# A row-wise maximum on one core: VectorE out of the opening barrier, one wait kept, a tail of 38 segments

## Chip, cores, metric

One core of a Trainium2 chip. The metric is device time in microseconds (us). The profile's span (first to last instruction of the kernel) is some 2.6 us shorter than the time.

## The reference

```python
def setup_inputs():
    return {"x": np.random.randn(8192, 8192).astype(np.float32)}

def reference(x):
    return np.linalg.norm(x, ord=np.inf, axis=1)
```

For a matrix, this norm along axis 1 is the largest absolute value of each row: 268 MB in, 32 KB out, one comparison per element.

## The kernel before

It walks through 32 tiles of 128 partitions with 16384 columns, two rows to a partition, in three buffers. The first 24 are loaded and reduced whole. The next seven ("the tail") are loaded in pieces of the widths in `TAIL`, and each piece is reduced as it lands, cut at the row's end (column 8192). The last tile has twelve pieces; its partial results are written beside the last piece of each row, so that one reduction closes the row.

```python
TAIL = [
    [4736, 11648],
    [12928, 3456],
    [7040, 9344],
    [9344, 7040],
    [3584, 6784, 6016],
    [5376, 4864, 1792, 4352],
    [4096, 3584, 3200, 2944, 2560],
]
LAST = (
    [(0, w) for w in (2176, 1792, 1792, 1664)]
    + [(1, w) for w in (1664, 1408, 1280, 1152, 1024, 896)]
    + [(0, 768), (1, 768)]
)
# ... cut: segments(), the passes on the finished program ...
def drop_implied_waits(nc):
    # ... cut: for loads on SP ...
        elif i.engine == dve and own and len(waits) > 1:
            past = max(behind.get((s.id, s.wait_value), 0) for s in waits)
            if past >= own:
                insts[n] = rewait(i, [s for s in waits if s.id != counter])
# ... cut ...
    for i, loads in enumerate(TAIL):
        t = sbuf.tile([P, W + PAD], F32, tag="t")
        # ... cut ...
        for j, w in enumerate(loads):
            nc.sync.dma_start(out=t[:, at : at + w], in_=x_t[i][:, at : at + w])
            at += w
            for _, b, c, n in [s for s in todo if s[0] == j]:
                k, lo = seen[b], b * cols + c
                absmax(part[:, i * B + b, k : k + 1], t[:, lo : lo + n])
                seen[b] += 1
```

The program opens with a barrier of all engines; one pass moves the first load ahead of it. The last two reductions each wait for two things, a load and VectorE's own counter; the first of these waits is an instruction of its own. In the trace of before the record of the last but one such wait is at 621.90 us (0.02 us long), while the reduction ahead still runs, to 622.20. What handles waits is called VectorE's sequencer here.

## Time and profile before

| | before |
|---|---|
| time, first three runs | 627.36, 627.47, 627.99 us |
| span of the profiled run | 624.7 us |
| load queue, share of 16 DMA engines | 99.6% |
| VectorE busy | 552.6 us (88%), 64 reductions |
| waits of VectorE for loads, 24 bulk tiles / tail | 70.6 us / 0.7 us |

The prediction shows the lines. In a timeline line the columns are: start, duration of the group, engine, source line, operation, output and input, shape of the first, count, and in brackets the idle time ahead of it and what ended it.

### The profile page before, as it was taken

Reading aid. Unit: us, or ns where it says so; the run is one execution under the profiler, and the core shown is the slowest. Engines: PE = TensorE matmul, PEld = TensorE weight load, DVE = VectorE, ACT = ScalarE, POOL = GpSimd, SP = SyncE. Lnnn points to the kernel's source line nnn. Section 1 sums busy time; section 2 is a strip of 40 time slices with the busy share of each in tenths; the row PEclk is TensorE's granted clock in tenths of the full one; section 3 lists DMA queues with packets and bytes.
Section 4 is the critical chain, followed back from the end, with each engine's and each line's share of the span. In section 5 each row is a group of like instructions: output and inputs, shape, how many; then the busy total and the mean of one; then the engine's idle time right before and its main releaser. Section 6 shows DMA issues by size and latency. Waiting matters only on the chain.

```text
span 624.7 us, 154 instructions
## 1 busy us (share of the span) xinstructions
DVE 552.6 (88%) x64; POOL 0.3 (0%) x5
## 2 busy tenths in 40 slices
DVE  0588988889988889888898888988889999999999
POOL 0000000000000000000000000000000000000000
DMA  9999999999999999999999999999999999999998
GB/s 403 457 415 457 415 449 424 441 432 411 462 403 470 403 470 403 453 420 449 424 445 428 415 457 403 470 403 470 403 427 446 424 430 438 418 434 429 425 425 340
DMA packets 8849, 268.47 MB, mean 430 GB/s; under 512 B 1680, under 2 KB 1680, under 8 KB 3216
## 3 DMA queue, kind: packets, MB, share of 16 engines
q1 hardware_dynamic: 8064, 268.44, 99.6%
q10 hardware_dynamic: 784, 0.02, 0.1%
q14 instruction: 1, 0.01, 0.0%
HBM read 268.44 MB, written 0.03 MB: 430 GB/s over the span
## 4 chain that ended last, share of the span: by engine, by line
DMA 64%; DVE 36%; issue 0%
DMA t<-in_x_dram 64%; DVE r_bulk L262 22%; DVE part L262 11%; DVE t L262 3%; DVE r_tail L262 0%
## 5 line engine op out<-in xcount | busy, mean ns | idle before, releaser
L262 DVE TENSOR_REDUCE r_bulk<-t 128x2 f32<-128x16384 f32 x24 | 413.3, 17220 | 70.6 <-DMA t<-in_x_dram 70.6
L262 DVE TENSOR_REDUCE part<-t 128x1 f32<-128x8192 f32 (+18 forms) x27 | 121.5, 4569 | 0.7 <-DMA t<-in_x_dram 0.7
L262 DVE TENSOR_REDUCE t<-t 128x1 f32<-128x1792 f32 (+7 forms) x10 | 16.2, 1687 | 0.0
L262 DVE TENSOR_REDUCE r_tail<-t 128x1 f32<-128x772 f32 (+1 forms) x2 | 1.8, 944 | 0.0
L262 DVE TENSOR_REDUCE r_tail<-part 128x14 f32<-128x42 f32 x1 | 0.2, 186 | 0.0
L259 POOL MEMSET part<- 128x42 f32 x1 | 0.1, 134 | 0.0
L343 POOL MEMSET const-bfloat16-1.0<- 128x1 bf16 x1 | 0.1, 102 | 0.0
L343 POOL MEMSET const-uint8-127<- 128x1 uint8 x1 | 0.1, 102 | 0.0
L343 POOL MEMSET const-float32-0.0<- 128x1 f32 x1 | 0.1, 98 | 0.2 <-issue 0.2
L343 POOL MEMSET const-float32-1.0<- 128x1 f32 x1 | 0.1, 98 | 0.0
## 6 DMA issues: line engine op xcount, KB each, us to landing
t<-in_x_dram SPq DMA_DIRECT2D x2, 4672.0 KB, 37.6
t<-in_x_dram SPq DMA_DIRECT2D x2, 3520.0 KB, 36.3
t<-in_x_dram SPq DMA_DIRECT2D x1, 6464.0 KB, 36.7
t<-in_x_dram SPq DMA_DIRECT2D x1, 5824.0 KB, 40.4
t<-in_x_dram SPq DMA_DIRECT2D x2, 1792.0 KB, 34.4
t<-in_x_dram SPq DMA_DIRECT2D x1, 3392.0 KB, 37.4
t<-in_x_dram SPq DMA_DIRECT2D x1, 3008.0 KB, 44.1
t<-in_x_dram SPq DMA_DIRECT2D x1, 2688.0 KB, 34.1
```

The costliest lines, as they stand in the source:

```text
L259: nc.gpsimd.memset(part[:], 0.0)
L262: return nc.vector.reduce_max(out=o, in_=i, axis=X, apply_absolute_value=True)
L343: nc = _bacc.Bacc("TRN2", target_bir_lowering=False, num_devices=1)
```

## The change

Its intent, as the diff reads, is to take from VectorE its part in the opening barrier (an announcement and a wait), and one segment of the tail (a segment is what one reduction takes; 39 before, 38 after). One wait that had been dropped as implied stays. The tail's widths are shuffled so that in the sixth tile a piece ends on the row's end.

```diff
 TAIL = [
-    [4736, 11648],
-    [12928, 3456],
+    [12672, 3712],
+    [4992, 11392],
     [7040, 9344],
     [9344, 7040],
     [3584, 6784, 6016],
-    [5376, 4864, 1792, 4352],
+    [3968, 4224, 4736, 3456],
     [4096, 3584, 3200, 2944, 2560],
 ]
@@ drop_implied_waits (cut: its bookkeeping lines, which go too)
-        elif i.engine == dve and own and len(waits) > 1:
-            past = max(behind.get((s.id, s.wait_value), 0) for s in waits)
-            if past >= own:
-                insts[n] = rewait(i, [s for s in waits if s.id != counter])
@@ new pass, run last
+def open_without_vector(nc):
+    dve, pool = mybir.EngineType.DVE, mybir.EngineType.Pool
+    main = nc.main_func.blocks[0]
+    out = []
+    for i in main.instructions:
+        kind = type(i).__name__
+        if i.engine == dve and kind in ("InstDrain", "InstEventSemaphore"):
+            continue
+        # ... cut: POOL's wait and release of the barrier count one less ...
+        out.append(i)
+    main.instructions = out
```

## The prediction

> **What bounds the kernel now.** I read the page first, top down: engines, slices, queues, chain, groups. The kernel streams 268.44 MB of float32 through 128-partition tiles of 16384 columns (24 "bulk" tiles of one load each, 8 "tail" tiles of several loads) and takes the largest absolute value per row on VectorE (DVE).

> ```profile
> span 624.7 us, 154 instructions
> DVE 552.6 (88%) x64; POOL 0.3 (0%) x5
> ...
> DMA  9999999999999999999999999999999999999998
> ...
> q1 hardware_dynamic: 8064, 268.44, 99.6%
> HBM read 268.44 MB, written 0.03 MB: 430 GB/s over the span
> ```

> To see here: in all 40 slices the DMA engines are at 90% or more, and the load queue alone keeps the sixteen engines 99.6% busy. VectorE has 12% to spare. The span is bytes divided by DMA rate, plus a short head and a short end.

> Second, the groups with shapes kept apart, and one stretch of the timeline, for the two speeds:

> ```profile
> L262 DVE TENSOR_REDUCE r_bulk<-t 128x2 f32<-128x16384 f32 x24 | 413.3, 17220 | 70.6 <-DMA t<-in_x_dram 70.6
> L262 DVE TENSOR_REDUCE part<-t 128x1 f32<-128x8192 f32 x4 | 34.7, 8681 | 0.2 <-DMA t<-in_x_dram 0.2
> L262 DVE TENSOR_REDUCE part<-t 128x1 f32<-128x1152 f32 x2 | 2.7, 1342 | 0.0
> ...
> 22.03 17.22 DVE L262 TENSOR_REDUCE r_bulk<-t 128x2 f32<-128x16384 f32 x1 [22.03 <-DMA t<-in_x_dram]
> ...
> 466.67 17.22 DVE L262 TENSOR_REDUCE r_bulk<-t 128x2 f32<-128x16384 f32 x1 [2.14 <-DMA t<-in_x_dram]
> ```

> To see here: from the first bulk reduction at 22.03 to the 24th at 466.67 there are 23 tiles in 444.64 us, 19.33 us each; VectorE needs 17.22 and waits about 2.1 us per tile for the DMA.

> Third, the tail, where the change lies:

> ```profile
> 483.81 17.33 DVE L262 TENSOR_REDUCE part<-t 128x1 f32<-128x4736 f32 x3
> 501.32 86.61 DVE L262 TENSOR_REDUCE part<-t 128x1 f32<-128x8192 f32 x18 [0.19 <-DMA t<-in_x_dram]
> 588.47 17.57 DVE L262 TENSOR_REDUCE part<-t 128x1 f32<-128x4096 f32 x6 [0.54 <-DMA t<-in_x_dram]
> 605.96 2.41 DVE L262 TENSOR_REDUCE t<-t 128x1 f32<-128x2176 f32 x1
> 608.28 0.19 DVE L262 TENSOR_REDUCE r_tail<-part 128x14 f32<-128x42 f32 x1
> 608.38 13.82 DVE L262 TENSOR_REDUCE t<-t 128x1 f32<-128x1792 f32 x9
> 622.12 1.81 DVE L262 TENSOR_REDUCE r_tail<-t 128x1 f32<-128x772 f32 x2
> 623.96 0.35 SPq L324 DMA_DIRECT2D out_dram<-r_tail  x1
> ```

> To see here: VectorE is nearly always busy here because it began the tail 17 us behind the data, but it still waits for data twice: 0.19 us at 501.32 and 0.54 us at 588.47. After 588.47 it runs to the end almost without a gap, one small load after another. So the end hangs on when the load at 588.47 and those after it land, and then on VectorE work after that. Work saved on VectorE before 588.47 cannot reach the end.

> Fourth, the waits of the queue that issues the loads, for the opening barrier, and the start of the chain of waits:

> ```profile
> SPq L343 <- PEq L343: 0.2, 1, 0.2
> ...
> 0.73 0.07 issue
> 0.80 40.50 DMA t<-in_x_dram
> ```

> To see here: the only wait of the issuing queue in the opening barrier is 0.2 us, put down to TensorE's sequencer and not to VectorE. It then issues the second load at 0.80.

> [...]8.389 MB per 19.33 us is 434 GB/s in the bulk. Nothing in the change can raise that. [...](8681 - 1342) ns over (8192 - 1152) columns is 1.042 ns a column[...], so a reduction costs about 1.042 ns per column plus 1342 - 1201 = 141 ns. [...]a reduction that reads what VectorE has just written starts at 608.28 and the next at 608.38, 0.10 us later. [...] The kernel before has two reductions (the last two) that wait for both a load and VectorE's own counter; the gap before each is at most 0.2 us.

> **The change part by part.**

> *1. VectorE out of the opening barrier.* Two small VectorE sequencer instructions go (its report and its wait), and the collector on POOL counts one fewer. The last to report was not VectorE, so the barrier opens at the same time[...]. Even the whole 0.80 us would gain nothing in the load stream: the first load is issued at 0.00, ahead of the barrier, and keeps all engines busy for about 20 us, so the second only has to be there by about 20. VectorE's first work is at 22.03. Effect on the end: 0.

> *2. A wait kept.* The pass no longer drops VectorE's wait on its own counter where the load waited for had itself been issued behind that count. The code puts such a wait on the first reduction of the last tile (it writes partial results into a reused buffer), so about 605.96. The count it asks for was reached when the buffer's former tile was done, about 570. [...] This stretch is the one that sets the end, so a cost would count fully. [...]

> *3. Tail splits.* The number of loads per tile does not change (2, 2, 2, 2, 3, 4, 5 and 12), nor the bytes. Only tiles 1, 2 and 6 have other widths. With about 1.19 us per 1000 columns (19.5 us per 16384):

> Tile 1, first load 12672 instead of 4736: lands at 466.65 + 15.0 = 481.7, still before VectorE is free at 483.81. Three segments as before. Effect 0.

> Tile 2, first load 4992 instead of 12928: it lands 9.4 us earlier, so the wait of 0.19 at 501.32 goes. VectorE comes to be 0.19 earlier, until the second load of tile 4, which it took up at 535.92 straight after other work; that load lands near there, so the 0.19 should come back as a wait there or later.

> Tile 6, segments 3968, 4224, 4736, 3456 instead of 5376, 2816, 2048, 1792, 4352: the new cut falls exactly on the row's end (3968 + 4224 = 8192), so four reductions do what five did. An extra segment costs (17.33 - 17.22)/2 = 0.055 us from tile 1, or (17.57 - 17.22)/5 = 0.07 from tile 7, because most of the 141 ns overlaps the neighbour. So 0.06 us less VectorE work. Loads land at about 568.3, 573.4, 579.1 and 583.2; reductions of 4.28, 4.54, 5.08 and 3.74 us then end near 587.7, against 583.25 + 4.68 = 587.93 before. The next load lands near 588.45 in both, since the bytes before it are the same. So the wait before it grows from 0.54 to about 0.75 and the end does not move.

> Sum: [...]about 0 us of 627.5.

> **The rivals.**

> *The kept wait holds VectorE.* [...] For it: there is no slack after 588.47. Against it: the count is some 35 us old.

> *VectorE sets the end throughout the tail.* Then both the 0.06 of a segment and the 0.19 of tile 2 would come off: about 627.2. For it: 156.5 us busy of the last 158.7. Against it: the wait of 0.54 at 588.47, which swallows both.

> *Other load sizes starve or slow the DMA.* Loads are issued when a buffer of the three comes free, and late in the tail when an earlier load of the same semaphore has landed. If one came too late, the stream would have a hole; a hole of 1 us would be 628.5. Against it: issue to landing of tail loads is mostly 30 to 45 us, so one or two whole tiles always stand in the queue; the buffers' releases move by less than 0.3 us. [...]

> *The barrier held the launch.* If VectorE in unprofiled runs reaches its first instruction late, leaving it out gains some tenths: 627.0 to 627.3. The trace doesn't show this, but time minus span (627.3 - 624.7) is not seen in the profile at all.

> **Range and chances.** Predicted 627.4 us. The three runs of before spread over 0.63 us, more than everything above adds up to[...]. A range of 626.6 to 628.2 is 627.4 plus or minus 0.8. 2% is 12.5 us: no part of the change has a path to that in either direction. Only an accident[...] could, so 0.5% for faster and 1% for slower.

> **What would show it right or wrong.** Right: DMA at 9 in all slices, 430 GB/s; bulk reductions still 19.33 us apart; no wait near 501; a wait of about 0.7 just before the 4096-column reduction, still at about 588.5; four reductions in tile 6; the last reductions at about 622.1 and 623.0; the second load issued within 0.05 us of 0.80. Wrong: the 4096-column reduction starting before 588.3 or after 588.8 (the load stream moved), a gap over 0.1 us around 606 (the kept wait costs), or a last reduction that starts other than 34.5 us after it.

The sum came to about 0 us of 627.5. Two terms, barrier and tail, were 0 each.

## The result, and the profile after

| | before | after |
|---|---|---|
| time, median of 6 fast runs | 627.62 us (627.36 to 628.06) | 627.42 us (627.25 to 628.14) |
| span of the profiled run | 624.7 us | 624.7 us |

The ratio is the mean time of one kernel's fast runs over that of the other's in the same rounds, so not quite the ratio of these medians: 0.9999, with a 95% interval of 0.9986 to 1.0012. That is the same time. A second set of five runs of the same text (run 6 below) gave 0.9996 (0.9984 to 1.0009).

So the forecast of 627.4 held. But its own list of signs did not. The page of after, engines, memory and groups (columns as in the prediction; line numbers have moved by 18):

```profile
span 624.7 us, 152 instructions
...
HBM read 268.44 MB, written 0.03 MB: 430 GB/s over the span
...
L280 DVE TENSOR_REDUCE part<-t 128x1 f32<-128x8192 f32 (+19 forms) x26 | 121.4, 4739 | 0.5 <-DMA t<-in_x_dram 0.5
...
L280 DVE TENSOR_REDUCE r_tail<-t 128x1 f32<-128x772 f32 (+1 forms) x2 | 1.8, 954 | 0.2 <-DVE t L280 0.2
```

One reduction fewer, 0.5 us of waiting for loads where before had 0.7, and a line that before did not have: a reduction near the end stood idle for 0.2 us, which the view puts down to VectorE itself. VectorE's timeline of after, the stretches that answer to those in the prediction:

```profile
466.75 17.22 DVE L280 TENSOR_REDUCE r_bulk<-t 128x2 f32<-128x16384 f32 x1 [2.13 <-DMA t<-in_x_dram]
...
536.01 8.69 DVE L280 TENSOR_REDUCE part<-t 128x1 f32<-128x8192 f32 x1 [0.31 <-DMA t<-in_x_dram]
...
588.20 17.61 DVE L280 TENSOR_REDUCE part<-t 128x1 f32<-128x4096 f32 x6 [0.23 <-DMA t<-in_x_dram]
605.73 2.41 DVE L280 TENSOR_REDUCE t<-t 128x1 f32<-128x2176 f32 x1
...
622.14 1.82 DVE L280 TENSOR_REDUCE r_tail<-t 128x1 f32<-128x772 f32 x2 [0.16 <-DVE t L280]
```

Measured from the start of the last bulk reduction, so that the stream's early history drops out, the 4096-column reduction starts after 588.20 - 466.75 = 121.45 us. In before it was 588.47 - 466.67 = 121.80. The load stream is 0.35 us ahead, although not a byte less is loaded. The load just ahead of this one was still level: its last completion came 116.52 us after the start of the last bulk reduction in both. Then the last but one reduction starts 0.16 us after the one ahead of it has ended, where back-to-back reductions start 0.08 us *before* the other's recorded end (in before 621.13 + 1.07 = 622.20 against 622.12). That is 0.24 us lost. Gain and loss nearly cancel: the last reduction starts 156.32 us after the last bulk one in before (622.99) and 156.26 in after (623.01).

Both show in the DMA view of a short window, which the prediction had not asked for. The page of before already had a queue named "instruction", with one packet. The DMA view of before, 586 to 588 us:

```profile
q1 hardware_dynamic: 69, 0.80, 96.6%
q14 instruction: 1, 0.01, 1.0%
```

and of after, the same window, then 622 us to the end:

```profile
q1 hardware_dynamic: 72, 0.85, 99.7%
...
q14 instruction: 1, 0.01, 1.5%
q1 hardware_dynamic: 6, 0.01, 1.2%
```

Columns: queue, packets, MB, share of sixteen engines in the window. To see: in before one read of instructions falls into the middle of the load stream, and the load queue's share drops from 99.7% to 96.6% for those two microseconds. (The drop is a rough sign: 93.2% in run 11, the same text as before, and 99.7% in run 3 over the window of its read.) In after this read comes at the end, when hardly a load is left. The packet's record gives 8192 bytes, starting at 586.95 us and taking 0.33 us in before, at 622.83 and 0.64 us in after. In before the last of the sixteen completions of the 4096-column load came 0.37 us after the one before it (0.06 us for the load just ahead): this reads as one DMA engine fallen behind, and the last completion stayed 0.3 us behind the others to the end.

**Rival B.** The tail's new widths moved the stream. **Rival C.** The read comes at a time of its own (for another engine or by chance), and the two profiles differ by luck.

### The profile page after: what moved, and what is told of

It reads as the page before. It is cut to its first block, busy times and chain, and to the rows that moved or that the text cites. A ratio compares the mean times of both kernels' runs of the same rounds, so it can differ in the third digit from the quotient of the medians.

```text
span 624.7 us, 152 instructions
## 1 busy us (share of the span) xinstructions
DVE 552.6 (88%) x63; POOL 0.3 (0%) x5
## 2 busy tenths in 40 slices
DMA  9999999999999999999999999999999999999998
## 3 DMA queue, kind: packets, MB, share of 16 engines
q1 hardware_dynamic: 8064, 268.44, 99.6%
HBM read 268.44 MB, written 0.03 MB: 430 GB/s over the span
## 4 chain that ended last, share of the span: by engine, by line
DMA 63%; DVE 36%; another core or an unknown queue 0%; DVEq 0%; issue 0%
DMA t<-in_x_dram 63%; DVE r_bulk L280 25%; DVE part L280 8%; DVE t L280 3%; DVEq L373 0%; DVE r_tail L280 0%
## 5 line engine op out<-in xcount | busy, mean ns | idle before, releaser
L280 DVE TENSOR_REDUCE r_bulk<-t 128x2 f32<-128x16384 f32 x24 | 413.3, 17220 | 70.7 <-DMA t<-in_x_dram 70.7
L280 DVE TENSOR_REDUCE part<-t 128x1 f32<-128x8192 f32 (+19 forms) x26 | 121.4, 4739 | 0.5 <-DMA t<-in_x_dram 0.5
```

The lines of the kernel that those rows point to most:

```text
L280: return nc.vector.reduce_max(out=o, in_=i, axis=X, apply_absolute_value=True)
```

## The experiments

Twelve runs, all correct. Those with no timed rounds are single runs, whose state is unknown; they are read from their profiles, and their single times (627.0 to 627.5 us) tell nothing at this size. The numbers, all from the traces: "65th" is what stands there in VectorE's program; "4096" is the start of the 4096-column reduction and "last" that of the last reduction, both from the start of the last bulk reduction; "gap" is idle time ahead of one of the last two reductions.

| kernel | VectorE's program against before | 65th instruction | read at, us | 4096, us | gap, us | last, us |
|---|---|---|---|---|---|---|
| before | 0 | last reduction of the 896 columns | 586.95 | 121.80 | none | 156.32 |
| before, run 11 | 0 | the same | 586.92 | 121.79 | none | 156.31 |
| after | -2 | last but one reduction | 622.83 | 121.44 | 0.16 | 156.25 |
| after, run 6 | -2 | the same | 622.97 | 121.46 | 0.16 | 156.26 |
| 1 barrier only | -2 | the same | 622.60 | 121.42 | 0.17 | 156.25 |
| 2 tail only | -1 | wait ahead of it | 591.88 | 121.42 | none | 156.42 |
| 3 wait only | +1 | reduction of the 1024 columns | 609.65 | 121.43 | none | 156.15 |
| 4 barrier, wait | -1 | wait ahead of the last but one | 609.44 | 121.41 | none | 156.27 |
| 5 short | -5 | branch after the last | 624.06 | 121.43 | none | 156.00 |
| 7 barrier, tail | -3 | wait ahead of the last | 623.45 | 121.43 | none | 156.00 |
| 8 thirty more | +30 | in the tail's third tile | 298.87 | 121.42 | none | 155.99 |
| 9 four fewer | -4 | the last reduction | 623.85 | 121.43 | 0.35 | 156.43 |
| 10 rows only | -3 | wait ahead of the last | 622.76 | 121.43 | none | 156.02 |
| 12 rows only, timed | -3 | the same | 623.43 | 121.96 | none | 156.56 |

### 1. Barrier only

```diff
+    nc.at_finalize(open_without_vector)
```

> Before with VectorE left out of the opening barrier and nothing else (VectorE's program two instructions shorter). Theory A (instruction read): a fixed place in VectorE's program, about its 65th instruction, sets off one read of 8 KB of instructions on one DMA engine; in before the sequencer runs ahead to it and the read falls into the load stream at 586.95 us, in after it lies behind the wait for the last but one load, and the read falls at 622.83. Two instructions fewer put the 65th behind that wait too: read at about 622.8, the 4096-column reduction 121.44 us after the last bulk reduction as in after (before: 121.80), although the tail is the old one. Rival B (tail widths move the stream): as before, 121.80. Rival C (the read comes at a time of its own): anywhere.

Measured: read at 622.60, 121.42 us with the old tail. Rival B falls with this. VectorE's timeline, last reductions:

```profile
621.93 1.82 DVE L289 TENSOR_REDUCE r_tail<-t 128x1 f32<-128x772 f32 x2 [0.17 <-DVE t L289]
```

The gap of after is here too, without the kept wait and without the new tail. Two instructions fewer, wherever they are taken, give the whole picture of after.

### 2. Tail only

```diff
-    [4736, 11648],
-    [12928, 3456],
+    [12672, 3712],
+    [4992, 11392],
-    [5376, 4864, 1792, 4352],
+    [3968, 4224, 4736, 3456],
```

> Before with the new tail widths only (one reduction fewer, 38 segments). Theory A: the 65th instruction is now the wait itself, which the sequencer still reaches by running ahead; read in the load stream near 588, landings after it about 0.35 us late, last reductions as in before. Rival B: the stream comes early as in after, 121.44 from the last bulk reduction to the 4096-column one. Rival C: anywhere.

The DMA view of this kernel from 591 to 593 us:

```profile
q1 hardware_dynamic: 78, 0.80, 96.6%
q14 instruction: 1, 0.01, 1.0%
```

and VectorE's timeline around it:

```profile
588.15 8.21 DVE L262 TENSOR_REDUCE part<-t 128x1 f32<-128x4096 f32 x2 [0.22 <-DMA t<-in_x_dram]
596.71 3.55 DVE L262 TENSOR_REDUCE part<-t 128x1 f32<-128x512 f32 x2 [0.35 <-DMA t<-in_x_dram]
```

A miss in part: the read is still in the stream, but at 591.88 and not near 588 as I had put it. It has moved by one reduction: in before it came 3.70 us after the start of the 4352-column reduction (583.25), here 3.73 us after that of the 4096-column one (588.15). In both programs that is the 48th instruction, so by inference from these two the sequencer is about 17 ahead; no trace counts it. Loads after the read are late (0.35 us of waiting at 596.71), those before it are not (121.42). My place for the read was off by 4 us because I had not allowed for the 3.7 us between the cause and the read; the theory stands. B, read as "the widths make the stream early", is not needed: 121.41 to 121.46 is what every run but 12 shows whose read does not fall ahead of that reduction in the tail.

### 3. Wait only

```diff
-        elif i.engine == dve and own and len(waits) > 1:
-            past = max(behind.get((s.id, s.wait_value), 0) for s in waits)
-            if past >= own:
-                insts[n] = rewait(i, [s for s in waits if s.id != counter])
```

> Before with the wait kept only (one more VectorE instruction, a wait that holds the sequencer until the load at about 605.7). Theory A: the sequencer cannot run past that wait, and then reaches the 65th at once: the read moves from 587 to about 606 to 609, so the 4096-column reduction comes 121.44 us after the last bulk one, and the lateness of about 0.3 us appears only after about 608; end as in before. Rival B: as before, 121.80. The kept wait itself: no gap over 0.05 us before the 2176-column reduction.

VectorE's timeline of this kernel around the kept wait:

```profile
603.08 2.81 DVE L258 TENSOR_REDUCE part<-t 128x1 f32<-128x2560 f32 x1
605.81 2.41 DVE L258 TENSOR_REDUCE t<-t 128x1 f32<-128x2176 f32 x1
```

The record of the kept wait is at 605.60, while the 2560-column reduction is still running; the next follows it without a gap (603.08 + 2.81 = 605.89, started at 605.81). So the wait itself left no gap here. The read did what the theory says: it moved from 586.95 to 609.65, 4 us after the wait ended. The lateness is smaller than I expected: the last reduction is at 156.15, where before has 156.32.

### 4. Barrier and wait, old tail

```diff
+    nc.at_finalize(open_without_vector)
-        elif i.engine == dve and own and len(waits) > 1:
-            ...
```

> Barrier without VectorE and wait kept, old tail of 39 segments (one VectorE instruction fewer than before, one more than after). Theory A: the 65th instruction is the wait for the last but one load; the sequencer is let past the kept wait at about 605.6 and reaches it at once, so the read falls at about 606 to 609 and the last loads land late by about 0.3 us: the segment fewer in after is what moves the read behind the last but one load. If instead this looks like after (read at 622.8), the place is one instruction later than I think.

Read at 609.44, no gap at the end, last reduction at 156.27. As expected: one instruction more than in after, and the read goes from 622.8 back into the stream.

### 5. A shorter program

```diff
 (barrier only and tail only, and)
-    [7040, 9344],
-    [9344, 7040],
+    [8192, 8192],
+    [8192, 8192],
```

> A shorter VectorE program than after by three: no kept wait, and 36 segments (tiles 3 and 4 loaded as two whole rows of 8192, so two reductions instead of three). Theory A: the 65th instruction now lies behind the last reduction, so no reduction waits for it; read after 622.8 or never, the 4096-column reduction 121.4 us after the last bulk one, and no gap before the last but one reduction (after: 0.16 us). The last reduction then starts at about 622.75 instead of 623.01, span about 624.45 against 624.72 (for a stream that starts alike). In time: about 0.25 us under after, under half of the run-to-run spread, so verdict same. If the gap of 0.16 stays, it does not come from the place in the program.

The gap is gone and the last reduction starts at 156.00, 0.25 us earlier than in after. The span did not show it: this run's stream reached the last bulk reduction at 466.94, 0.19 us later than in after, and the end came to 622.94 and 624.66 instead of the 622.75 and 624.45 that I had named. Time over five rounds: 627.19 us (627.15 to 627.53) against 627.54 of before, ratio 0.9993 (0.9981 to 1.0006): the same.

### 6. After again

> After, word for word, for a second profile and more timed runs. Theory A: read at 622.8 plus or minus 0.1 again, 121.44 us again, gap of about 0.16 before the last but one reduction again, time 627.3 within 0.5 and same as before. Rival C (the read comes at a time of its own): elsewhere.

Read at 622.97, 121.46 us, the gap of 0.16 again. Time 627.45 us, the same. Together with run 11 this rules out C: the read repeats to within 0.15 us in both texts.

### 7. After without the kept wait

```diff
 (after, with these lines and their bookkeeping put back)
+        elif i.engine == dve and own and len(waits) > 1:
+            past = max(behind.get((s.id, s.wait_value), 0) for s in waits)
+            if past >= own:
+                insts[n] = rewait(i, [s for s in waits if s.id != counter])
```

> The change without the kept wait (one VectorE instruction fewer than after). Theory A: the 65th instruction is now the wait for the last load, behind the last but one reduction: read at about 622.8, 121.4 us as in after, no gap before the last but one reduction but perhaps one of up to 0.25 us before the last, so the end between that of the short kernel and that of after. Time the same within noise; the kept wait would then have been needless.

VectorE's timeline, the last two reductions:

```profile
622.50 1.82 DVE L289 TENSOR_REDUCE r_tail<-t 128x1 f32<-128x772 f32 x2
```

No gap ahead of either of the two, last reduction at 156.00, time 627.05 us (627.00 to 627.72), ratio 0.9989 (0.9976 to 1.0003): not clear of noise. The place now falls on the wait for the last load, which had to stand until that load anyway. So the kept wait is not only needless here: as one instruction more it puts the place on a reduction and gives the gain back (156.25 in after).

### 8. Thirty small writes ahead

```diff
+    # ... cut: a pass that looks for POOL's write is told to pass over these
+    idle = outp.tile([P, 30], F32)
+    for k in range(30):
+        nc.vector.memset(idle[:, k : k + 1], 0.0)
```

> Before with 30 one-element writes on VectorE ahead of the first reduction, where it idles for 22 us. Theory A: the 65th instruction is now 30 earlier in the work. In before and in the kernel with the tail alone, the read came 3.7 us after the start of the 48th instruction; here the 48th is bulk reduction 15, which starts at about 292.7, so the read at about 296.4, and one spacing of bulk reductions of up to 19.66 instead of 19.33 just after it. No read near 587; the 4096-column reduction 121.4 us after the last bulk one. The end as in before within 0.2 us[...]. Rival C: read near 587 as before.

VectorE's timeline of this kernel in the bulk:

```profile
292.87 17.22 DVE L269 TENSOR_REDUCE r_bulk<-t 128x2 f32<-128x16384 f32 x1 [2.14 <-DMA t<-in_x_dram]
312.39 17.22 DVE L269 TENSOR_REDUCE r_bulk<-t 128x2 f32<-128x16384 f32 x1 [2.30 <-DMA t<-in_x_dram]
```

and the DMA view from 298 to 300 us:

```profile
q14 instruction: 1, 0.01, 1.0%
```

The read has moved by 288 us, into the bulk, six us after the 48th instruction started (expected 3.7). That spacing of bulk reductions is 19.52 us; the same spacing in before is 19.35, so this read seems to have cost 0.17 us (0.15 in run 3, up to 0.42 in run 2). One such spacing is weak evidence: runs 5 and 7 each have one of 19.54 or 19.55 early on with no read near. From there on nothing is late: 155.99 us at the end, because the loss lies ahead of the last bulk reduction. I had written up to 0.33 for the cost, and "the end as in before within 0.2 us"; the end, at 623.04 against 622.99, is, but the two runs already differ by 0.39 us where the tail begins.

### 9. Four fewer

```diff
 (barrier only and tail only, and)
-    [7040, 9344],
+    [8192, 8192],
```

> Barrier without VectorE, no kept wait, 37 segments: VectorE's program four instructions shorter than before, between the kernel without the kept wait (three shorter, no gap) and the short one (five shorter, no gap). Theory A: the 65th instruction is now the last reduction itself, right behind the wait for the last load: read at about 622.8 to 623.5, no gap before the last but one reduction, but one of 0.1 to 0.3 us before the last, so that the last starts about 156.2 us after the last bulk one (156.0 in those two neighbours, 156.26 in after). If there is no gap, what delays a reduction in after is not that it is the 65th instruction.

VectorE's timeline, the last three reductions, here on three lines because of the gap:

```profile
620.89 1.08 DVE L289 TENSOR_REDUCE t<-t 128x1 f32<-128x896 f32 x1
621.89 0.95 DVE L289 TENSOR_REDUCE r_tail<-t 128x1 f32<-128x772 f32 x1
623.19 0.96 DVE L289 TENSOR_REDUCE r_tail<-t 128x1 f32<-128x774 f32 x1 [0.35 <-DVE r_tail L289]
```

This is the sharpest of the twelve. Three fewer have no gap, five fewer have none, and four fewer have one of 0.35 us ahead of exactly the reduction that is the 65th instruction. It came out larger than I said (0.1 to 0.3), and the last reduction, at 156.43, is the latest of all but run 12. What holds it there no trace shows; what is shown is that the reduction at this place, and no other, is late.

The trace's records of VectorE's waits show how late. Wherever a reduction is the 65th (after, runs 1, 6 and 9), it starts 0.48 us after the record of the wait ahead of it (here 622.71, then 623.19); in runs 7 and 10, where it is not, the last reduction starts 0.06 us after its wait. The delay is thus the same in after and here, and the gap is what the reduction ahead did not cover: in after it still ran for 0.31 us, here for 0.13. So the larger gap is no larger delay.

### 10. Rows only

```diff
 (tail only, and)
-    [7040, 9344],
-    [9344, 7040],
+    [8192, 8192],
+    [8192, 8192],
```

> Before with 36 segments (tails as in the short kernel), VectorE still in the opening barrier, no kept wait: three instructions fewer than before, all of them taken from the tail. Theory A: only the count matters, so as the kernel with barrier and 38 segments: no read inside the load stream, 121.4 us from the last bulk reduction to the 4096-column one, last reduction 156.0 us after the last bulk one. If leaving VectorE out of the barrier has a gain of its own, this one should be later than that.

VectorE's timeline from the 4096-column reduction on, and its last two reductions:

```profile
588.09 17.62 DVE L262 TENSOR_REDUCE part<-t 128x1 f32<-128x4096 f32 x6 [0.28 <-DMA t<-in_x_dram]
...
621.78 1.85 DVE L262 TENSOR_REDUCE r_tail<-t 128x1 f32<-128x772 f32 x2
```

With VectorE in the barrier as in before, three instructions fewer do what they do without it: 156.02 against 156.00. Leaving VectorE out of the barrier shows no gain of its own.

### 11. Before again

> Before, word for word, for a second profile. Theory A: read at 587 plus or minus 1 again, about 3.7 us after the 4352-column reduction starts; the slowest engine's loads after it late by 0.15 to 0.4 us; last reduction 156.2 to 156.35 us after the last bulk one. Rival C: read elsewhere.

The DMA view from 586 to 588 us:

```profile
q1 hardware_dynamic: 67, 0.77, 93.2%
q14 instruction: 1, 0.01, 1.0%
```

Read at 586.92, 121.79 and 156.31 us: as in the first profile of before.

### 12. Rows only, timed

> The kernel with 36 segments and nothing else changed, once more, now timed in five rounds. Theory A: no read in the load stream, no gap before the last two reductions, last reduction 156.0 us after the last bulk one, 0.3 us earlier than in before and 0.25 earlier than in after; time about 627.1 to 627.3 against 627.5 of before, the interval of the ratio still holding 1 because single runs of one kernel spread by up to 1 us; verdict same.

VectorE's timeline of this run in the tail:

```profile
483.93 60.35 DVE L262 TENSOR_REDUCE part<-t 128x1 f32<-128x8192 f32 x9
544.94 43.51 DVE L262 TENSOR_REDUCE part<-t 128x1 f32<-128x8192 f32 x9 [0.66 <-DMA t<-in_x_dram]
```

A miss in this profile: 121.96 and 156.56. The read is at the end, as it should be (623.43), and there is no gap at the last two. What is late is the stream itself, and that before 544.94: near 509 us eight packets of 32 KB, all under way at the same time, took 0.6 to 0.9 us more than the 1.2 us that is the median of their size in the tail's first half. Nothing of the kind is in run 10, the same text. Where that comes from is open; it is of the size of the spread between runs of one kernel. Time: 627.51 us (627.14 to 627.71) against 627.57, ratio 0.9997 (0.9984 to 1.0011): the same.

## Why the prediction was right or wrong

*Bound by the load stream, nothing in the change to move 2%:* right. 430 GB/s and 99.6% in both.

*Barrier, 0:* right. The second load is issued at 0.80 us in both, and run 10 against run 7 shows no gain of its own. Nor is there one ahead of the profile's span, as the rival on the launch had it: time minus span is 2.59 to 2.65 us in the six runs of after, and 2.59 to 2.68 in the nine of before that run 5 was timed against.

*Kept wait, next to nothing where it stands:* right as far as the wait itself goes (run 3: no gap, the next reduction starts 0.08 us before the recorded end). That it also shifts everything behind it by one place in the program was not seen.

*Tile 2, wait of 0.19 gone and back as a wait at the load of 535.9:* right, with 0.31 measured there.

*Tile 6, wait before the 4096-column reduction growing to 0.75 because "the next load lands near 588.45 in both, since the bytes before it are the same":* wrong, and this is the step that failed. The wait shrank to 0.23: counted from the last bulk reduction, the load came 0.36 us earlier than forecast and VectorE was free 0.17 later. The smaller part lies in the forecast's own sum: its 587.7 is 587.93 less 0.06 for the segment and 0.19 for tile 2, but the 0.19 had already come back as a wait at tile 4. The larger part is the load. The bytes loaded were the same, but the DMA engines had also moved 8 KB of instructions, one packet of 0.33 us, and from then on the last of each load's sixteen completions came about that much behind the others (0.37 us, then 0.30 to 0.34). The page of before had a line for that queue, which the prediction did not quote; it carried 0.0% and I did not ask when it fell.

*The last reduction 34.5 us after the 4096-column one:* wrong, 34.81. Of the 0.29 us more, 0.24 is the reduction that stands at the 65th place, and 0.04 lies ahead of 600 us.

*The sum, about 0:* right in value, and to that extent by luck, for two terms that nearly cancel were both missing: about -0.35 from the read, about +0.29 given back. Either term alone is under 0.1% of the time. The rival "VectorE sets the end throughout the tail" is not what happened; the rival "other sizes slow the DMA" neither (121.42 with the old tail, 121.44 with the new). No rival named instructions.

What stays open: why a read costs 0.15 to 0.42 us in the stream. Its packet takes 0.31 to 0.33 us there; on what the cost depends no run shows. Open too is why the reduction at the 65th place is late, and why the read comes 3.7 to 6.0 us after the start of the 48th instruction in the stream (before, runs 2 and 8) and 1.17 us after the wait at the end (after: 621.66, 622.83). And the best kernels here (runs 5, 7 and 10, though not 12, which is the text of 10) start their last reduction 0.25 us earlier than after and 0.3 earlier than before, counted from the last bulk reduction, while the timed rounds of 5, 7 and 12 cannot tell any of them from before.

## What to carry to other kernels

This kernel keeps its DMA engines full (99.6%), and one packet that no line of the source asks for moved its tail by 0.15 to 0.42 us: when a queue of the profile shows one packet, ask for the window in which it fell. VectorE's program here has a place that goes with one read of 8192 bytes of instructions; the number of instructions ahead of it decided whether that fell into the load stream, onto a critical instruction or into a wait, and that can undo or fake a gain of some tenths of a microsecond. When a change is worth less than the spread of single runs, measure it from an event inside the trace, not from the time.
